# A hybrid layer on one core: the mask inside the scan, w_out prepared in another phase, ten working tiles

## The chip, the cores and the metric

One Trainium2 chip, one of its cores. The program is launched once and runs the whole layer. The metric is the device time of one execution in microseconds, as the median of several runs. TensorE (PE) multiplies and transposes into PSUM, VectorE (DVE) and ScalarE (ACT) work on SBUF and PSUM, GpSimd (POOL) works on SBUF and starts stores, SyncE (SP) starts loads. Each of these engines takes its instructions in the order in which they stand in its own queue.

## The reference

One layer on 2048 positions of width 1024, all float32. A modulated copy of the input, `h = x * (1 + scale) + shift`, goes through one projection into seven groups of 512 columns. Three feed a gated MLP (`u`, `v`, `z_a`), four feed an attention of 8 heads of width 64 (`q`, `k`, `v_b`, `z_b`).

```python
mod = c @ w_ada + b_ada                        # shift, scale, gate
h = x * (1 + scale) + shift
u_a, v_a, z_a, q_b, k_b, v_b, z_b = split(h @ w_in, 7)
out_a = gelu(u_a) * (w_spatial_masked @ layer_norm(gelu(v_a)) + b_s) * silu(z_a)

z = q @ k.T / 8                                # per head, blocks of 128 queries
valid = s_pos < t_pos                          # strictly causal
log_keep = where(valid, -softplus(z), 0)
after = reverse_cumsum(log_keep) - log_keep
w = where(valid, exp(log_sigmoid(z) + after), 0)
out_b = (w @ v_b) * silu(z_b)

y = concat(out_a, out_b) @ w_out
out = layer_norm(2**0.25 * x + (1 + gate) * y, ln_g, ln_b)
```

The attention has no softmax: each key takes a share `sigmoid(z)` of what the keys behind it have left over. In product form `keep = sigmoid(-z)` is what a key leaves, and the running product of `keep` from the newest key to the oldest is what remains.

## The kernel before

**Arithmetic.** Every product of two matrices is made of three matmuls of a high and a low part (`split`, L62: a CAST makes the high part, mostly on ACT, L65, and a subtraction on DVE makes the low part, L68). A step of a projection is three matmuls of 512 columns into one PSUM tile.

**Phases of projection work.** The 2048 positions are four chunks of 512. First `k` and `v_b` of all chunks are made, then `q` and `z_b` of chunk 0 (`qz_chunk`, L226). From there on PE's queue is written as two interleaved streams: the attention, as units, and the rest of the projections, as `pieces` (L899): `q`/`z_b` of chunks 1 to 3 (phases q1, q2, q3), then `v_a` and the spatial mixing (va), then `u` and `z_a` (uz, `gmlp_uz`, L603), then the output projection and the norm (out). The PSUM tiles of these are named `pqz`, `pva`, `puz` and `po` in the rows below.

**An attention unit** (`Unit`, L775) is one head, 256 queries and one chunk of 512 keys. It makes `z` on PE (L805, L806), `kp = sigmoid(-z)` on ACT (L809), for the diagonal chunk a mask on POOL (L812, it writes 1 where the key is not before the query), the running product by a scan on DVE (L820), a transposition on PE into `tr` (L835), the split of that into `wth` and `wtl` (L65, L68), and the product with the values into `pv` (L852, L854), which DVE adds into `ot` (L868). Units are a few steps apart in PE's queue: while one is at its scores, the one before is at its scan and the one before that at its transposition.

**What sets the order.** For PE the order is written out by hand (L944 to L968): a table `rate` (L925) says how many nanoseconds of projection work go beside an attention unit of a given size in each phase. For `k`, `v_b` and the first `q`/`z_b` chunk the orders of SP, DVE and ACT are the written ones too. Elsewhere a scheduler orders the other engines' queues. A tile of a pool takes over the buffer of an earlier one when that one's last reader is done.

**The preparation of w_out** (`prep_out`, L202) is a generator: it loads a block of 128 rows of `w_out` into a `raw` tile by SP (L206), multiplies it by the gate (L213), splits each half into `woh` and `wol`, and stores both parts by POOL into the scratch tensor `wo_d` (L218, L219). There are 8 blocks. `qz_chunk` of chunks 0 and 1 drives it, at the steps listed in L239. The output phase reads `wo_d` back.

**Shared buffers.** `r2` (L103) is a pool of 8 tiles of 128x512: the `sz`, `eh_q`, `el_q` of the q phases, `woh` and `wol`, gelu's two tiles (`gv`, `gt`, `gu`, `gtu`), the mixing result (`mx`, `mxl`), silu's `sga` and the split output `oh`, `ol`. `raw4` (L97) is a pool of 3 tiles of 128x1024, for weights before their split and for rows of `x` later. The gate stays in one of them from the end of the k/v phase to the end of `prep_out`.

**gelu** (L183) copies its PSUM input to SBUF on ACT, squares the PSUM input on ACT (L185), goes on with DVE (L186), a sigmoid on ACT (L187) and DVE (L188).

Of the kernel before, what the change touches and what calls it, by code (L numbers as in the profile page):

```python
# [9 lines left out]
F32 = mybir.dt.float32  # L10
# [25 lines left out]
def layer_kernel(ctx: ExitStack, tc: tile.TileContext, x, c, w_ada, b_ada, w_in, ln_v_g, ln_v_b,  # L36
# [20 lines left out]
    mb_d = [dram.tile([P, 2, 4, CH], F32, name=f"mb_d{i}") for i in range(NC)]  # L57
    wo_d = dram.tile([2, 4, P, 2, 2, 512], F32, name="wo_d")

    store = nc.gpsimd  # L60
# [20 lines left out]
    zero = const.tile([P, 1], F32, name="zero")  # L81
    nc.vector.memset(zero, 0.0)
    cb = const.tile([3 * NB, P], F32, name="cb")
    nc.scalar.dma_start(cb[0:NB], c.rearrange("(b p) -> b p", p=P))
# [18 lines left out]
    def r2(nm, dt=F32, shape=(P, 512)):  # L103
        return right.tile(list(shape), dt, tag="t2", bufs=8, name=nm)

# [77 lines left out]
    def gelu(t, dst, src):  # L183
        nc.scalar.copy(dst, src)
        nc.scalar.activation(t, src, AF.Square)  # L185
        nc.vector.scalar_tensor_tensor(t, t, GC2, dst, op0=ALU.add, op1=ALU.mult)  # L186
        nc.scalar.activation(t, t, AF.Sigmoid, scale=GSC)  # L187
        nc.vector.tensor_tensor(dst, dst, t, op=ALU.mult)  # L188
# [13 lines left out]
    def prep_out():  # L202

        def load(b):
            raw = raw4(f"woraw_{b}", (P, D))
            nc.sync.dma_start(raw, w_out[b * P:(b + 1) * P, :])  # L206
            return raw

        raws = [load(0), load(1)]
        yield 0  # L210
        for b in range(NB):
            raw = raws[b]
            nc.vector.tensor_tensor(raw, raw, gates[0], op=ALU.mult)  # L213
            for i in range(2):
                cs = slice(i * 512, (i + 1) * 512)
                hi, lo = r2(f"woh_{b}_{i}", F32R), r2(f"wol_{b}_{i}", F32R)
                split(hi, lo, raw[:, cs], "act")
                store.dma_start(wo_d[i, b // 2][:, b % 2, 0, :], hi.bitcast(F32))  # L218
                store.dma_start(wo_d[i, b // 2][:, b % 2, 1, :], lo.bitcast(F32))  # L219
            if b + 2 < NB:  # L220
                raws.append(load(b + 2))
            yield 0

    gates, prep, kept = [], [], [None]

    def qz_chunk(ci, hts, w_q, w_z):  # L226
# [9 lines left out]
        tiles += [(w_z, m, True, lambda acc, m=m: put_z(m, acc)) for m in range(4)]  # L236
        for i, ns in enumerate(project(hts, tiles, f"pqz_{ci}", ci > 0, 0 < ci < NC - 1)):
            yield ns
            if ci < 2 and i in ((26, 36, 44, 52, 60), (7, 23, 39, 55))[ci]:  # L239
                yield next(prep[0], 0)  # L240


    with ExitStack() as sa:
# [80 lines left out]
        def make_gate():  # L324
# [16 lines left out]
            gate = raw4("gate", (P, D))  # L341
            gates.append(gate)
            bg = raw4("bgate", (P, D))
            nc.sync.dma_start(bg, b_ada[2 * D:3 * D].unsqueeze(0).broadcast_to([P, D]))
            yield 0
            for i in range(2):
                cs = slice(i * 512, (i + 1) * 512)
                gp = pj(f"gp_{i}")
                nc.tensor.matmul(gp, ones, gacc[:, cs], start=True, stop=True)
                nc.vector.scalar_tensor_tensor(gate[:, cs], gp, 1.0, bg[:, cs], op0=ALU.add, op1=ALU.add)  # L350
                yield 0

        def put_k(ci, m, acc):
# [122 lines left out]
        with tc.manual_schedule(engines={ET.PE, ET.SP, ET.DVE, ET.Activation}):  # L476
# [38 lines left out]
            w_steps = split_steps(w_z, G_ZB, "z", 2)  # L515
            prep.append(prep_out())
            for i, _ in enumerate(qz_chunk(0, hts, w_q, w_z)):
# [85 lines left out]
    def gmlp_uz():  # L603
        w_u = []
        u_steps = split_steps(w_u, G_U, "u")
        for ci in range(NC):
# [38 lines left out]
            for i, ns in enumerate(project(hts, tiles, f"puz_{ci}", ci > 0, ci < NC - 1)):  # L645
                yield ns
                if ci == 0 and i in (6, 8, 18, 25, 28):
                    next(u_steps)

    def turn_a(ci, t, mx):  # L650
# [124 lines left out]
    class Unit:  # L775
# [23 lines left out]
        def scores(self):  # L799
# [8 lines left out]
            for js, w_ in self.rng:  # L808
                nc.scalar.activation(self.kp[:, js, 0:w_], z[:, js, 0:w_], AF.Sigmoid, scale=-ZSC)  # L809
            for j in range(2) if self.diag else ():  # L810
                own = self.kp[:, j, self.wid[j] - P:self.wid[j]]
                nc.gpsimd.affine_select(own, own, pattern=[[-1, P]], compare_op=ALU.is_gt, fill=1.0, base=0,  # L812
                                        channel_multiplier=1)

        def remains(self):

            kp = self.kp
            for j in range(2):
                w_ = self.wid[j]
                nc.vector.tensor_tensor_scan(kp[:, j, 0:w_][:, ::-1], kp[:, j, 0:w_][:, ::-1],  # L820
                                             zero.broadcast_to([P, w_]),
                                             1.0 if self.diag else self.prev.kp[:, j, 0:1],
                                             op0=ALU.mult, op1=ALU.add)

# [74 lines left out]
    def pieces():  # L899
        for ci in range(1, NC):  # L900
# [3 lines left out]
            done.add(ci)  # L904
        yield from prep.pop()
        phase[0] = "va"
# [17 lines left out]
    left = dict(q1=64 * 648, q2=64 * 648, q3=64 * 648, va=128 * 648 + 1800 + 16 * 660, uz=256 * 648 + 32 * 224, out=210 * 648)  # L924
    rate = dict(q1=4.1, q2=3.3, q3=3.3, va=9.0, uz=3.9, out=4.8)  # L925
    stream = with_waiting(pieces())
# [69 lines left out]
```

## Time and profile before

| | |
|---|---|
| median of three runs | 1312.83 us (1311.06 to 1313.43) |
| the profiled execution | 1313.83 us, its span 1312.1 us |
| mean granted TensorE clock | 0.986 of full speed |
| busy share of the span | PE 95%, DVE 72%, ACT 43%, POOL 24% |
| bytes moved | 269.23 MB, 205 GB/s on average |

PE is busy almost everywhere, so a time saved elsewhere counts only where PE waits for it. Matmuls are pipelined: a busy PE may still run at half clock, which the granted clock of a stretch tells. The span has three parts in which PE has real gaps: the start (until about 60 us), the q phases (about 250 to 390 us) and some places between 580 and 775 us; at the end the last norm and store follow the last matmul.

### The profile page before, as it was taken

The page shows a single profiled execution, that of the slowest core. Times are in us where ns is not written, and L with a number is a line of the kernel's source. Part 1 is how long each engine was busy: PE and PEld are TensorE (multiplying, and loading weights), DVE is VectorE, ACT ScalarE, POOL GpSimd, SP SyncE. Part 2 cuts the span into 40 slices and gives each one's busy share as a digit, 9 for nine tenths or more (in the row PEclk, how much of TensorE's full clock was granted, in tenths as well). Part 3 has the DMA queues.
Part 4 walks back from the last instruction along what each step waited for, and adds up shares of the span by engine and source line. Part 5 has one row for each costly group of instructions (what it writes and reads, how often), then busy time and mean ns, then how long its engine had stood idle before and what let it go on. Part 6 is the DMA issues. An engine that isn't in the chain of part 4 may idle for free.

```text
span 1312.1 us, 18828 instructions
## 1 busy us (share of the span) xinstructions
PE 1245.6 (95%) x6678; PEld 1054.7 (80%) x6678; DVE 949.2 (72%) x1362; ACT 561.8 (43%) x1079; POOL 310.6 (24%) x540
## 2 busy tenths in 40 slices
PE   4999999888899999999989989999999999999997
PEld 4788877677678888888868868888888887888885
DVE  6633453446677787878798878888788778878874
ACT  3333222223344454455565545555454433444330
POOL 1344333243222211345431111111001112111111
PEclk9999999999899999999999989999999999999999
DMA  9699876899975764654455653753775976565331
GB/s 318 220 372 320 283 265 203 313 334 306 306 217 167 235 185 134 212 193 153 129 169 177 198 165 102 218 138 110 214 235 137 309 206 185 163 176 168 105 121 49
DMA packets 174623, 269.23 MB, mean 205 GB/s; under 512 B 15008, under 2 KB 107200, under 8 KB 174528
## 3 DMA queue, kind: packets, MB, share of 16 engines
q1 hardware_dynamic: 147216, 178.30, 45.8%
q0 software_dynamic: 27264, 89.70, 19.6%
q8 instruction: 53, 0.87, 0.3%
q14 instruction: 42, 0.34, 0.1%
q10 hardware_dynamic: 48, 0.01, 0.0%
HBM read 180.37 MB, written 83.36 MB: 201 GB/s over the span
## 4 chain that ended last, share of the span: by engine, by line
PE 68%; DVE 10%; issue 9%; DMA 5%; POOL 4%; ACT 2%; SPq 1%; POOLq 0%; DVEq 0%; ACTq 0%
PE puz_False L160 12%; PE pkv L160 11%; PE po L694 10%; PE pqz_True L160 7%; PE tr L835 7%; PE pv L854 4%; PE pv L852 4%; PE z L806 4%; PE z L805 4%; DVE kp L820 2%; PE pva_False L160 2%; DMA woraw<-in_w_out_dram 1%; DMA ht_qz<-ht_d 1%; DVE macc L306 1%; PE pk L160 1%
## 5 line engine op out<-in xcount | busy, mean ns | idle before, releaser
L65 ACT CAST wth<-tr 128x512 fp32r<-128x512 f32 (+2 forms) x352 | 170.8, 486 | 258.1 <-PE tr L835 167.5
L820 DVE TENSOR_TENSOR_SCAN kp<-kp,kp,zero 128x512 f32<-128x512 f32 x192 | 240.0, 1277 | 53.2 <-ACT kp L809 52.9
L68 DVE TENSOR_TENSOR wtl<-tr,wth 128x512 fp32r<-128x512 f32 (+2 forms) x352 | 194.2, 561 | 33.0 <-ACT wth L65 30.2
L694 PE MATMUL po<-wo,mt 128*128 128x512 f32 x744 | 197.5, 402 | 0.7 <-DVE xr L704 0.6
L809 ACT ACTIVATE kp<-z 128x128 f32<-128x128 f32 (+3 forms) x224 | 148.0, 691 | 106.0 <-PE z L806 105.6
L835 PE MATMUL tr<-ident,kp 128*128 128x128 f32 x1088 | 170.7, 277 | 9.1 <-DVE kp L820 8.0
L694 PEld LDWEIGHTS po<-wo,mt 128*128 128x128 f32 x744 | 133.7, 189 | 26.2 <-DVE xr L704 1.6
L835 PEld LDWEIGHTS tr<-ident,kp 128*128 128x128 f32 x1088 | 129.2, 141 | 28.6 <-DVE kp L820 9.5
L852 PE MATMUL pv<-wth,vs 128*128 128x256 f32 x576 | 142.3, 279 | 2.6 <-DVE ot L868 2.6
L854 PE MATMUL pv<-wtl,vs 128*128 128x256 f32 x576 | 141.6, 284 | 0.6 <-DVE wtl L68 0.6
L820 DVE TENSOR_TENSOR_SCAN kp<-kp,zero 128x128 f32<-128x128 f32 (+3 forms) x128 | 103.6, 836 | 34.1 <-POOL kp L812 32.3
L852 PEld LDWEIGHTS pv<-wth,vs 128*128 128x128 f32 x576 | 110.4, 192 | 10.5 <-DVE ot L868 3.9
L805 PE MATMUL z<-ks,qt 128*128 128x512 f32 (+2 forms) x320 | 115.7, 367 | 1.6 <-issue 1.2
L806 PE MATMUL z<-ks,qt 128*128 128x512 f32 (+2 forms) x320 | 117.0, 365 | 0.0
L854 PEld LDWEIGHTS pv<-wtl,vs 128*128 128x128 f32 x576 | 110.5, 192 | 7.2 <-DVE wtl L68 0.8
L812 POOL TENSOR_SCALAR_AFFINE_SELECT kp<-kp 128x128 f32<-128x128 f32 x128 | 49.7, 402 | 214.1 <-ACT kp L809 212.5
L160 PE MATMUL puz_False<-wh_u,ht_uz 128*128 128x512 f32 x192 | 77.1, 422 | 1.8 <-ACT gtu L185 1.8
L160 PE MATMUL pqz_True<-ht_qz,wh_q 128*128 128x512 f32 x192 | 72.0, 413 | 6.9 <-DVE sz L181 3.2
L160 PE MATMUL pqz_True<-ht_qz,wh_z 128*128 128x512 f32 x192 | 74.7, 416 | 3.2 <-DVE el_q L68 3.2
L160 PE MATMUL pkv<-wh_v,hta 128*128 128x512 f32 x224 | 75.8, 402 | 0.5 <-DVE el_k L68 0.5
L160 PE MATMUL puz_False<-wh_za,ht_uz 128*128 128x512 f32 x192 | 75.0, 413 | 0.0
L805 PEld LDWEIGHTS z<-ks,qt 128*128 128x128 f32 x320 | 60.5, 189 | 13.0 <-issue 2.4
(203 smaller groups left out, 2338.9 us busy)
## 6 DMA issues: line engine op xcount, KB each, us to landing
ks<-k_d SPq DMA_DIRECT2D x160, 128.0 KB, 4.1
vs<-v_d SPq DMA_DIRECT2D x80, 256.0 KB, 3.9
qt<-q_d SPq DMA_DIRECT2D x64, 256.0 KB, 4.6
ht_d<-hta POOLq DMA_DIRECT2D x24, 512.0 KB, 5.5
ht_qz<-ht_d SPq DMA_DIRECT2D x24, 512.0 KB, 11.6
ht_va<-ht_d SPq DMA_DIRECT2D x24, 512.0 KB, 4.9
ht_uz<-ht_d SPq DMA_DIRECT2D x24, 512.0 KB, 6.0
wada<-in_w_ada_dram SPq DMA_DIRECT2D x32, 256.0 KB, 6.6
```

The costliest lines, as they stand in the source:

```text
L65: nc.scalar.copy(hi, src)
L68: (sub or nc.vector).tensor_tensor(lo, src, hi.bitcast(F32), op=ALU.subtract)
L160: nc.tensor.matmul(acc, l_, r_, start=(b == 0 and i == 0), stop=(b == NB - 1 and i == 2))
L694: nc.tensor.matmul(acc, ms[l_], w[:, r_, :], start=(b == 0 and i == 0), stop=(b == NB - 1 and i == 2))
L805: nc.tensor.matmul(z[:, j, 0:w_], hd.q[:, 0, qs], hd.k[self.s][:, 0:w_], start=True, stop=False)
L806: nc.tensor.matmul(z[:, j, 0:w_], hd.q[:, 1, qs], hd.k[self.s][:, 0:w_], start=False, stop=True)
L809: nc.scalar.activation(self.kp[:, js, 0:w_], z[:, js, 0:w_], AF.Sigmoid, scale=-ZSC)
L812: nc.gpsimd.affine_select(own, own, pattern=[[-1, P]], compare_op=ALU.is_gt, fill=1.0, base=0, channel_multiplier=1)
L820: nc.vector.tensor_tensor_scan(kp[:, j, 0:w_][:, ::-1], kp[:, j, 0:w_][:, ::-1], zero.broadcast_to([P, w_]), 1.0 if self.diag else self.pr ...
L835: nc.tensor.transpose(tp[:, e, j * P:(j + 1) * P], self.kp[:, j, kb * P:(kb + 1) * P], ident)
L852: nc.tensor.matmul(self.pv[:, cs], hd.v[self.s][:, kb, :], self.wt[0][:, kb, cs], start=self.diag and kb == 0, stop=False)
L854: nc.tensor.matmul(self.pv[:, cs], hd.v[self.s][:, kb, :], self.wt[1][:, kb, cs], start=False, stop=self.s == 0 and kb == self.nkb - 1)
```

## The change

It has five parts.

1. The mask on POOL (L812) goes. A constant tile `least` is 0 where the key is before the query and 1 where not; the diagonal scan's second operation is now a maximum with `least` in place of an addition of zero. As no `keep` exceeds 1, the running product stays at 1 through the masked keys and then goes on as before.
2. `prep_out` is driven from `gmlp_uz` and no longer from `qz_chunk`: its first loads at step 36 of chunk 0, then one call at every 16th step of chunks 1 to 3, which makes the 8 blocks in chunks 1 and 2. The gate waits in a scratch tensor `gate_d` and is loaded into a `raw` tile when it is needed.
3. `r2` has 10 buffers in place of 8.
4. gelu's square reads the copy in SBUF in place of the PSUM tile.
5. In `rate`, q2 and q3 go from 3.3 to 3.2, uz from 3.9 to 4.2 and out from 4.8 to 4.6.

```diff
+    gate_d = dram.tile([1, D], F32, name="gate_d")
...
+    least = const.tile([P, CH], F32, name="least")
+    nc.gpsimd.memset(least, 0.0)
+    nc.gpsimd.affine_select(least[:, CH - P:CH], least[:, CH - P:CH], pattern=[[-1, P]], compare_op=ALU.is_gt, fill=1.0,
+                            base=0, channel_multiplier=1)
...
-        return right.tile(list(shape), dt, tag="t2", bufs=8, name=nm)
+        return right.tile(list(shape), dt, tag="t2", bufs=10, name=nm)
...
-        nc.scalar.activation(t, src, AF.Square)
+        nc.scalar.activation(t, dst, AF.Square)
...
+        gate = raw4("gate_all", (P, D))
+        nc.sync.dma_start(gate, gate_d.broadcast_to([P, D]))
         raws = [load(0), load(1)]
-        yield 0
+        yield
         for b in range(NB):
             raw = raws[b]
-            nc.vector.tensor_tensor(raw, raw, gates[0], op=ALU.mult)
+            nc.vector.tensor_tensor(raw, raw, gate, op=ALU.mult)
...
-            if ci < 2 and i in ((26, 36, 44, 52, 60), (7, 23, 39, 55))[ci]:
-                yield next(prep[0], 0)
+        yield from project(hts, tiles, f"pqz_{ci}", ci > 0, 0 < ci < NC - 1)
...
+            nc.gpsimd.dma_start(gate_d, gate[0:1, :])
...
-        u_steps = split_steps(w_u, G_U, "u")
+        u_steps, wo_steps = split_steps(w_u, G_U, "u"), prep_out()
...
+                if ci == 0 and i == 36 or ci and i % 16 == 9:
+                    next(wo_steps, None)
...
-            for j in range(2) if self.diag else ():
-                own = self.kp[:, j, self.wid[j] - P:self.wid[j]]
-                nc.gpsimd.affine_select(own, own, pattern=[[-1, P]], compare_op=ALU.is_gt, fill=1.0, base=0,
-                                        channel_multiplier=1)
...
-                nc.vector.tensor_tensor_scan(kp[:, j, 0:w_][:, ::-1], kp[:, j, 0:w_][:, ::-1],
-                                             zero.broadcast_to([P, w_]),
-                                             1.0 if self.diag else self.prev.kp[:, j, 0:1],
-                                             op0=ALU.mult, op1=ALU.add)
+                keep = kp[:, j, 0:w_][:, ::-1]
+                if self.diag:
+                    nc.vector.tensor_tensor_scan(keep, keep, least[:, CH - w_:CH][:, ::-1], 1.0, op0=ALU.mult, op1=ALU.max)
+                else:
+                    nc.vector.tensor_tensor_scan(keep, keep, zero.broadcast_to([P, w_]), self.prev.kp[:, j, 0:1],
+                                                 op0=ALU.mult, op1=ALU.add)
...
-        yield from prep.pop()
...
-    rate = dict(q1=4.1, q2=3.3, q3=3.3, va=9.0, uz=3.9, out=4.8)
+    rate = dict(q1=4.1, q2=3.2, q3=3.2, va=9.0, uz=4.2, out=4.6)
```

What this moves in the queues is shown at two places. The first is VectorE's queue where `q` and `z_b` of chunk 0 end. `pqz` is the PSUM tile of a projection, `el_q` and `sz` are what DVE makes of it, `woraw` and `wol` belong to w_out. Before:

```order
L68 TENSOR_TENSOR el_q_3_1989<-pqz_3_True_1945,eh_q_3_1988 128x512
L213 TENSOR_TENSOR woraw_1969<-woraw_1969,gate 128x1024
L68 TENSOR_TENSOR wol_0_2012<-woraw_1969,woh_0_2011 128x512
L68 TENSOR_TENSOR wol_1_2018<-woraw_1969,woh_1_2017 128x512
L181 TENSOR_TENSOR sz_0_2034<-pqz_0_True_1994,sz_0_2034 128x512
L213 TENSOR_TENSOR woraw_1971<-woraw_1971,gate 128x1024
L68 TENSOR_TENSOR wol_0_2056<-woraw_1971,woh_0_2055 128x512
L68 TENSOR_TENSOR wol_1_2062<-woraw_1971,woh_1_2061 128x512
L181 TENSOR_TENSOR sz_1_2078<-pqz_1_True_2038,sz_1_2078 128x512
```

The same place in the changed kernel:

```order
L69 TENSOR_TENSOR el_q_3_1992<-pqz_3_True_1952,eh_q_3_1991 128x512
L186 TENSOR_TENSOR sz_0_2022<-pqz_0_True_1997,sz_0_2022 128x512
L186 TENSOR_TENSOR sz_1_2051<-pqz_1_True_2026,sz_1_2051 128x512
L186 TENSOR_TENSOR sz_2_2080<-pqz_2_True_2055,sz_2_2080 128x512
L186 TENSOR_TENSOR sz_3_2109<-pqz_3_True_2084,sz_3_2109 128x512
L69 TENSOR_TENSOR el_q_0_2170<-pqz_0_True_2128,eh_q_0_2169 128x512
```

Each `sz` stood behind the multiplication of a block of w_out, and now the reads of PSUM stand one behind the other.

The second place is ScalarE's queue where chunk 2 of the uz phase begins. `puz` is the PSUM tile of `u` or `z_a`, `gu` and `gtu` are gelu's tiles, `oh` is the split output of chunk 1, `kp`, `wth` and `hv` belong to attention units. Before:

```order
L65 CAST wth_7_0_1_8472<-tr_7_0_1_1_8494 128x512
L809 ACTIVATE kp_7_1_2_8512<-z_7_1_2_8507 128x384
L809 ACTIVATE kp_7_1_2_8512<-z_7_1_2_8507 128x512
L65 CAST wth_7_0_0_8529<-tr_7_0_0_0_8531 128x512
L65 CAST oh_3_8543<-oT_3_8538 128x512
L184 COPY gu_0_8551<-puz_0_False_8351 128x512
L185 ACTIVATE gtu_0_8552<-puz_0_False_8351 128x512
```

The same place in the changed kernel:

```order
L66 CAST oh_2_8100<-oT_2_8095 128x512
L66 CAST woh_0_8114<-woraw_7641 128x512
L814 ACTIVATE kp_7_0_1_8111<-z_7_0_1_8106 128x1024
L66 CAST woh_1_8120<-woraw_7641 128x512
L66 CAST wth_7_0_2_8141<-tr_7_0_2_0_8143 128x256
L66 CAST wth_7_0_2_8141<-tr_7_0_2_0_8143 128x128
L66 CAST oh_3_8164<-oT_3_8159 128x512
L189 COPY gu_0_8172<-puz_0_False_7980 128x512
L190 ACTIVATE gtu_0_8173<-gu_0_8172 128x512
```

Two casts of w_out have moved in ahead of the copy that frees `puz`, and the square behind that copy reads `gu` and not `puz`. In the built program `gu_0_8172` takes over the buffer of `woh_0_8114`.

## Rows read from the trace of the kernel before

**Rows 1.** Windows, q phases: length, busy of PE, PEld, DVE, ACT, POOL, PEclk, DMA, GB/s

```profile
250.00:390.00 140.00, 119.10 (x591) 98.05 (x590) 82.89 (x137) 51.37 (x136) 44.78 (x94) 0.94 0.96 298
263.05:266.45 3.40, 3.40 (x8) 2.70 (x9) 2.37 (x3) 1.14 (x2) 2.37 (x6) 0.53 0.88 217
307.20:310.20 3.00, 3.00 (x8) 2.43 (x9) 1.88 (x2) 0.00 (x0) 1.58 (x4) 0.51 1.14 262
353.03:358.40 5.37, 5.37 (x19) 4.69 (x20) 1.64 (x4) 1.20 (x3) 0.00 (x0) 0.50 1.04 346
```

**Rows 2.** Waits of PE from 240 to 390: us in total, times, longest

```profile
PE pqz_True L160 <- DVE sz L181: 9.8, 2, 6.6
PE pqz_True L160 <- DVE el_q L68: 4.0, 2, 3.2
PE pqz_True L160 <- DMA ht_qz<-ht_d: 2.9, 2, 1.5
PE pv L852 <- DVE ot L868: 2.6, 3, 1.3
```

**Rows 3.** Waits of DVE in the same stretch

```profile
DVE woraw L213 <- DMA woraw<-in_w_out_dram: 26.8, 5, 12.5
DVE kp L820 <- POOL kp L812: 14.6, 17, 3.4
```

**Rows 4.** DMA from 240 to 370: count, KB each, median us to landing

```profile
DMA packets 19432, 41.06 MB, mean 316 GB/s; under 512 B 2220, under 2 KB 7646, under 8 KB 19423
...
ht_qz<-ht_d SPq DMA_DIRECT2D x13, 512.0 KB, 13.2
...
woraw<-in_w_out_dram SPq DMA_DIRECT2D x8, 512.0 KB, 7.2
wo_d<-woh POOLq DMA_DIRECT2D x16, 256.0 KB, 7.3
```

**Rows 5.** Chain that ended last, 225 to 400: start, length, what

```profile
337.03 15.95 DMA ht_qz<-ht_d
```

**Rows 6.** Groups by line, whole span: busy, mean ns, idle before, releaser

```profile
L820 DVE TENSOR_TENSOR_SCAN kp<-kp,zero 128x128 f32<-128x128 f32 (+3 forms) x128 | 103.6, 836 | 34.1 <-POOL kp L812 32.3
L213 DVE TENSOR_TENSOR woraw<-woraw,gate 128x1024 f32<-128x1024 f32 x8 | 9.8, 1221 | 26.8 <-DMA woraw<-in_w_out_dram 26.8
L68 DVE TENSOR_TENSOR wol<-woraw,woh 128x512 fp32r<-128x512 f32 x16 | 10.4, 688 | 4.7 <-ACT woh L65 3.0 <-DMA wo_d<-woh 1.4
L65 ACT CAST woh<-woraw 128x512 fp32r<-128x512 f32 x16 | 9.3, 619 | 26.1 <-DVE woraw L213 21.3 <-DMA wo_d<-woh 4.1 <-DMA zb_d<-sz 0.7
L187 ACT ACTIVATE gtu<-gtu 128x512 f32<-128x512 f32 x16 | 10.1, 633 | 8.9 <-DVE gtu L186 8.9
L185 ACT ACTIVATE gtu<-puz_False 128x512 f32<-128x512 f32 x16 | 9.8, 611 | 2.0 <-DMA ma_d<-oh 2.0
```

**Rows 7.** Windows of the uz phase

```profile
662.00:690.00 28.00, 23.43 (x134) 19.25 (x134) 25.63 (x36) 18.07 (x36) 10.71 (x12) 1.00 0.53 156
753.00:775.00 22.00, 15.62 (x79) 13.04 (x78) 14.85 (x22) 8.36 (x16) 2.03 (x4) 0.84 0.47 153
767.12:771.10 3.98, 3.98 (x14) 3.30 (x14) 3.09 (x4) 0.58 (x1) 0.00 (x0) 0.50 0.17 66
780.00:940.00 160.00, 160.00 (x939) 139.13 (x938) 136.72 (x187) 84.61 (x162) 20.75 (x36) 1.00 0.57 166
```

**Rows 8.** Waits from 740 to 775

```profile
PE tr L835 <- DVE kp L820: 4.6, 1, 4.6
...
ACT gu L184 <- DMA ma_d<-oh: 3.1, 1, 3.1
```

**Rows 9.** DMA from 690 to 1020, stores of the split output

```profile
ma_d<-oh POOLq DMA_DIRECT2D x14, 256.0 KB, 3.7
```

**Rows 10.** Groups of DVE by line, 780 to 940

```profile
L820 DVE TENSOR_TENSOR_SCAN kp<-kp,kp,zero 128x512 f32<-128x512 f32 x42 | 52.1, 1272 | 12.1 <-ACT kp L809 12.0
L68 DVE TENSOR_TENSOR wtl<-tr,wth 128x512 fp32r<-128x512 f32 (+2 forms) x64 | 36.8, 588 | 5.6 <-ACT wth L65 5.1
```

More of the change, by code (lines that the diff above doesn't have):

```diff
@@ L221, in prep_out @@
                 raws.append(load(b + 2))
-            yield 0
-    gates, prep, kept = [], [], [None]
+            yield
+    kept = [None]
     def qz_chunk(ci, hts, w_q, w_z):
@@ L236, in qz_chunk @@
         tiles += [(w_z, m, True, lambda acc, m=m: put_z(m, acc)) for m in range(4)]
-        for i, ns in enumerate(project(hts, tiles, f"pqz_{ci}", ci > 0, 0 < ci < NC - 1)):
-            yield ns
-            if ci < 2 and i in ((26, 36, 44, 52, 60), (7, 23, 39, 55))[ci]:
-                yield next(prep[0], 0)
+        yield from project(hts, tiles, f"pqz_{ci}", ci > 0, 0 < ci < NC - 1)
     with ExitStack() as sa:
@@ L341, in make_gate @@
             gate = raw4("gate", (P, D))
-            gates.append(gate)
             bg = raw4("bgate", (P, D))
@@ L515, in layer_kernel @@
             w_steps = split_steps(w_z, G_ZB, "z", 2)
-            prep.append(prep_out())
             for i, _ in enumerate(qz_chunk(0, hts, w_q, w_z)):
```

## The prediction

> **What bounds the kernel now.** I read the windows first, then PE's waits, then the groups by line. In the windows the reader is to compare PE's busy time with the length. In the long stretch of the uz phase PE is busy for all of its 160.00 us at the full clock [rows 7]: there the kernel is bound by PE, and a saved microsecond on another engine is worth nothing. From 250 to 390 us PE is busy for 119.10 of 140.00 us, so 20.9 us are idle [rows 1]. The waits of the same stretch name them: 9.8 us for `sz` and 4.0 us for `el_q`, both DVE's reads of PSUM, 2.9 us for the hidden states `ht_qz`, 2.6 us for `ot` [rows 2], and 1.6 us that is left for small ones. [...] PE's queue keeps its work and nearly its order, and PE is the bound on both sides of the stretch, so I count what goes here one to one.
>
> Why DVE was late: its queue stands still for 26.8 us for blocks of `w_out`, once for 12.5 us [rows 3], with `sz` and `el_q` behind the waiting multiplication, and PE behind these, as PSUM has two tiles for projections. DMA is full there (0.96 busy [rows 1]); the 8 loads and 32 stores of w_out are 8 x 0.5 + 32 x 0.25 = 12 of the 41.06 MB moved from 240 to 370 us [rows 4].
>
> **w_out out of the q phases.** The waits for `sz` and `el_q` go with their cause: 13.8 us, and the first two slow stretches behind them, (3.40 + 3.00) / 2 = 3.2 us. That is 17.0 us, and I count all of it. What is late next is a transfer: one `ht_qz` took 15.95 us from issue [rows 5], against a median of 13.2 [rows 4], and PE needs these tiles some 11 to 13 us after they are issued (it waited 1.5 us at the longest). Without the 12 MB the queue ahead of it is shorter by three tenths, which brings 15.95 to about 11. So of the 2.9 us, the 1.6 us and the third slow stretch (2.7 us), 7.2 us in all, I count 6. Bounds: 0 and 7.2.
>
> **The mask.** 128 POOL instructions go. DVE waited 14.6 us for them in this stretch [rows 3], mostly where it was idle anyway; what PE saw of it is within the 2.6 us for `ot`. I count 1 us, between 0 and 2.6. The diagonal scan now takes a maximum with a tile, which no row shows. Its own group has 836 ns for 320 elements on average [rows 6]. At best it stays (nothing gets shorter, the elements are as many). At worst the second tile costs what a plain pass over two inputs costs, 688 ns x 320/512 = 430 ns [rows 6], and 128 of them add 55 us to DVE, of which only what falls in a full DVE would count. I take 0, as the addition already is a second operation of this row.
>
> [...]
>
> The tile `least` costs POOL two instructions at the start, where PE waits for the first loads. `gate_d` costs one small store and one load of 0.5 MB, in a phase with DMA to spare (0.57 [rows 7]).
>
> **w_out into the uz phase.** Each of 8 blocks costs DVE 1.22 us for the product and 2 x 0.688 us, ACT 2 x 0.619 us [rows 6], and four stores by POOL: 20.8 us of DVE and 9.9 us of ACT in all, over chunks 1 and 2, some 165 us. ACT has 84.61 of 160.00 us busy and takes it. DVE has 136.72 [rows 7]. By the table `rate`, attention leaves this phase: PE's queue has 226 transposes of 128 columns in chunks 1 and 2 before and 214 now, 5% fewer, which takes 5% of the scans and splits, (52.1 + 36.8) x 0.053 = 4.7 us [rows 10]. DVE then stands at 136.7 + 20.8 - 4.7 = 152.8 of 160 us, 95%. The cover is thin. Lower bound 0: at 85% PE did not wait at all. Upper bounds: if no idle time of DVE can be used, 20.8 us. If PE loses the share that it lost from 662 to 690 us, where DVE was busy for 25.63 of 28.00 us and PE for 23.43 [rows 7], 16% of 160 us is 26. That row had weights to split just ahead of their use, which here nobody waits for until the out phase, so I stay nearer to the 160 us row and take 5 us.
>
> What queues behind a waiting instruction: SP's load of block b + 2 waits for block b's buffer, with keys and values behind it, but these are issued a unit ahead. In SP's queue of the q phase, six of these loads stood ahead of the first keys and now three loads of `v_a`'s weights do.
>
> **Two more tiles, and the square.** From 753 to 775 us PE is idle for 22.00 - 15.62 = 6.4 us and at half speed for another 3.98 [rows 7], so 8.4 us are lost. It begins with ACT, which waits 3.1 us to copy a PSUM tile, as its target still holds a split output on its way to memory; PE then waits 4.6 us for the scan behind that [rows 8]. With 10 buffers such a reuse comes later, and the square no longer needs the PSUM tile (0.5 us earlier free). But 32 tiles of w_out join the pool. I count 5 us, between 0 and 8.4. The square costs ACT 633 in place of 611 ns [rows 6], 32 times, 0.7 us under cover.
>
> The out phase takes some of the attention that left: DVE rises there, PE has the same work in sum. I put 1 us against it, between 0 and 3.
>
> **Sum.** Gains 17.0 + 6 + 1 + 5 = 29, costs 5 + 1 = 6: 23 us. The profiled execution took 1313.8 us with a span of 1312.1; 1313.8 - 23 = 1290.8. The profiled one stands 1.0 us above the median shown, so the median should be about 1290.
>
> **Rivals.** [...]
>
> (b) DVE becomes the bound in chunks 1 and 2. With 12 us lost there in place of 5, and 3 of the 6 us of the transfer gained, it is 23 - 7 - 3 = 13, or 1300; with all 20.8 us lost and nothing gained from the transfer, 23 - 15.8 - 6 = 1, which is no change. For it: the row from 662 to 690 us.
>
> (c) Slower: the stall of 753 us at every block. If ACT has to wait for a w_out store before it can copy a PSUM tile, each such place costs 8.4 us [rows 7, 8]; 23 / 8.4 = 2.7, so from three of them on the gain is gone, and with four it is 1290 + 4 x 8.4 = 1324. For it: in ACT's queue a copy of `gu` stands five instructions behind the `woh` whose buffer it takes. Against it: it is the only reuse of that closeness that I found among the stored tiles, and stores in this phase land in 3.7 us where w_out's took 7.3 [rows 4, 9].
>
> [...]
>
> (d) The change does not do what it says: PE in the q phases meets another wait of the same size, the loads of keys and hidden states above all, as DMA stays full. Then 1312. Against it: the waits that go have their cause in w_out by name.
>
> **Chances.** The forecast with its near range, 1282 to 1296: 0.58. (a) 0.13. (b) 0.16. (c) 0.07. (d) 0.06. A difference under 0.2%, 2.6 us, is about what a measurement of this kernel cannot tell from none. Faster is forecast, (a) and (b), 0.87; within 0.2% most of (d), 0.05; slower (c) and a rest, 0.08. The range of 8 in 10 leaves out (c), (d) and the ends of (a) and (b): 1276 to 1305.
>
> **What would show it.** Right: PE idle from 245 to 365 us in the new profile at 5 us or less, the clock at 1.00 there, no wait of `pqz` for `sz`; DVE at 93 to 97% in chunks 1 and 2 of the uz phase, PE idle there under 6 us; mean diagonal scan within 3% of 836 ns. Wrong: PE waits for `ht_qz` over 4 us (then the transfer term fails); ACT waits for `wo_d` stores ahead of `gu` or `sga` (then (c)); PE waits for `tr` or `pv` from DVE all through chunks 1 and 2 (then (b)).

## The result and the profile after

The changed kernel takes 1289.7 us in the median of four runs (1289.29 to 1292.41), the one before 1311.9 (1309.23 to 1313.43) beside it: a ratio of 0.9843, 95% interval 0.9822 to 0.9864. The forecast was 1290 with 1276 to 1305. The profiled execution has a span of 1288.1 us, 24.0 less than before.

The windows below cut both spans at the same four pieces of work: the q phases (with the first `q`/`z_b` chunk), va, uz, out. First the kernel before, as length, then busy time of PE, PEld, DVE, ACT and POOL, granted clock, DMA share, GB/s:

```profile
221.90:517.80 295.90, 275.00 (x1454) 231.36 (x1452) 196.28 (x296) 125.14 (x285) 78.27 (x159) 0.97 0.77 242
517.80:656.80 139.00, 135.76 (x727) 115.50 (x726) 111.53 (x167) 73.38 (x166) 60.59 (x85) 0.99 0.58 177
656.80:1019.30 362.50, 351.54 (x2045) 303.89 (x2045) 303.69 (x414) 193.75 (x363) 56.21 (x93) 0.99 0.57 171
1019.30:1312.10 292.80, 280.62 (x1526) 238.48 (x1524) 228.34 (x320) 102.04 (x170) 40.89 (x83) 0.99 0.54 163
```

The same four of the changed kernel, and behind them the stretch of [rows 1] and chunks 1 and 2 of the uz phase:

```profile
222.80:493.60 270.80, 268.86 (x1469) 228.87 (x1467) 178.22 (x279) 120.30 (x276) 39.00 (x69) 1.00 0.69 218
493.60:632.30 138.70, 136.11 (x738) 115.78 (x738) 112.92 (x169) 77.94 (x167) 59.49 (x72) 1.00 0.57 181
632.30:982.00 349.70, 339.57 (x1960) 292.72 (x1959) 301.74 (x416) 190.63 (x360) 57.83 (x85) 1.00 0.69 207
982.00:1288.10 306.10, 289.16 (x1585) 245.26 (x1583) 238.29 (x333) 108.17 (x182) 35.13 (x65) 0.99 0.52 160
...
250.00:390.00 140.00, 138.90 (x751) 118.19 (x750) 84.13 (x145) 56.76 (x150) 17.85 (x33) 1.00 0.75 232
...
721.50:893.00 171.50, 165.56 (x951) 142.68 (x950) 152.58 (x214) 93.91 (x180) 34.34 (x57) 0.99 0.72 224
```

The q phases are 25.1 us shorter: 19.0 us less idle time of PE (20.9 to 1.9), and the mean granted clock is 1.00 in place of 0.97. The uz phase is 12.8 us shorter and the out phase 13.3 longer, which is mostly attention moved by the table: uz idles 10.1 us (11.0 before), out 16.9 (12.2). Here a phase's length misleads when work has moved; its idle time and its clock don't.

What answers to [rows 2] and [rows 4]: waits of PE from 240 to 390 (us in total, times, longest), then DMA from 240 to 370 (count, KB each, median us to landing), changed kernel:

```profile
PE z L810 <- DMA qt<-q_d: 0.9, 1, 0.9
PE pv L855 <- DVE ot L871: 0.2, 1, 0.2
```

```profile
DMA packets 19212, 33.30 MB, mean 256 GB/s; under 512 B 1952, under 2 KB 9120, under 8 KB 19203
...
ht_qz<-ht_d SPq DMA_DIRECT2D x8, 512.0 KB, 6.7
```

The waits for `sz`, `el_q` and `ht_qz` are gone, and hidden states land in 6.7 us in place of 13.2. Of the groups by line of the changed kernel, those that answer to [rows 6] (busy, mean ns, idle before and its releasers):

```profile
L823 DVE TENSOR_TENSOR_SCAN kp<-kp,least 128x128 f32<-128x128 f32 (+3 forms) x128 | 100.4, 820 | 15.2 <-ACT kp L814 14.5
L190 ACT ACTIVATE gtu<-gu 128x512 f32<-128x512 f32 x16 | 10.1, 634 | 2.2 <-DMA wo_d<-woh 1.0 <-DMA ma_d<-ol 0.9
L220 DVE TENSOR_TENSOR woraw<-woraw,gate_all 128x1024 f32<-128x1024 f32 x8 | 9.8, 1220 | 9.4 <-DMA woraw<-in_w_out_dram 7.5 <-issue 1.9
```

The scan with a maximum takes what the scan with an addition took, 820 ns against 836 [rows 6]. The product by the gate still waits for its load, 7.5 us in sum. That wait reaches PE. Waits of PE for DVE in the uz phase of the changed kernel, nearly all of its 10.1 us there:

```profile
PE pv L855 <- DVE ot L871: 5.3, 4, 2.1
PE tr L838 <- DVE kp L825: 3.9, 3, 2.4
```

DVE's and then PE's queue of the changed kernel around the longest one (start, duration, line, operation, in brackets the idle time before and its end):

```profile
832.42 1.22 DVE L220 TENSOR_TENSOR woraw<-woraw,gate_all 128x1024 f32<-128x1024 f32 x1 [4.13 <-DMA woraw<-in_w_out_dram]
...
836.54 2.45 DVE L825 TENSOR_TENSOR_SCAN kp<-kp,kp,zero 128x512 f32<-128x512 f32 x2
```

```profile
837.88 0.33 PE L838 MATMUL tr<-ident,kp 128*128 128x128 f32 x1 [2.44 <-DVE kp L825]
839.05 0.55 PE L838 MATMUL tr<-ident,kp 128*128 128x128 f32 x3 [0.85 <-DVE kp L825]
```

SP issued this load at 825.08, and the product stood at the head of DVE's queue from 828.3. The scan that PE needed stood six instructions behind it, and DVE had no gap between the two. With 0.57 us for `ot` at 834.76, which stood behind the product too, PE loses 3.9 us at this place, and in the 7 us from 836 on the granted clock is 0.76 on average.

### The profile page after: what moved, and what is told of

It reads as the page before. It is cut to its first block, busy times and chain, and to the rows that moved or that the text cites. A ratio compares the mean times of both kernels' runs of the same rounds, so it can differ in the third digit from the quotient of the medians.

```text
span 1288.1 us, 18465 instructions
## 1 busy us (share of the span) xinstructions
PE 1236.7 (96%) x6678; PEld 1048.2 (81%) x6678; DVE 940.6 (73%) x1362; ACT 564.5 (44%) x1079; POOL 267.6 (21%) x415
## 4 chain that ended last, share of the span: by engine, by line
PE 69%; DVE 13%; issue 9%; POOL 3%; DMA 3%; ACT 3%; SPq 0%; POOLq 0%; DVEq 0%; ACTq 0%
PE pqz_True L165 13%; PE pkv L165 11%; PE po L699 9%; PE puz_False L165 9%; PE tr L838 6%; PE pv L857 4%; PE pva_False L165 4%; PE z L810 3%; PE pv L855 3%; PE z L811 3%; DVE kp L825 3%; DVE wtl L69 2%; DVE macc L310 1%; PE pk L165 1%; PE xT L274 1%
## 5 line engine op out<-in xcount | busy, mean ns | idle before, releaser
L855 PEld LDWEIGHTS pv<-wth,vs 128*128 128x128 f32 x576 | 109.4, 190 | 13.8 <-DVE ot L871 7.7
L823 DVE TENSOR_TENSOR_SCAN kp<-kp,least 128x128 f32<-128x128 f32 (+3 forms) x128 | 100.4, 820 | 15.2 <-ACT kp L814 14.5
L165 PE MATMUL puz_False<-wh_u,ht_uz 128*128 128x512 f32 x192 | 74.5, 413 | 0.0
L810 PEld LDWEIGHTS z<-ks,qt 128*128 128x128 f32 x320 | 60.2, 188 | 14.8 <-ACT kp L814 3.0
L811 PEld LDWEIGHTS z<-ks,qt 128*128 128x128 f32 x320 | 60.3, 188 | 10.8
```

Of the source, the lines that this page charges most:

```text
L165: nc.tensor.matmul(acc, l_, r_, start=(b == 0 and i == 0), stop=(b == NB - 1 and i == 2))
L810: nc.tensor.matmul(z[:, j, 0:w_], hd.q[:, 0, qs], hd.k[self.s][:, 0:w_], start=True, stop=False)
L811: nc.tensor.matmul(z[:, j, 0:w_], hd.q[:, 1, qs], hd.k[self.s][:, 0:w_], start=False, stop=True)
L823: nc.vector.tensor_tensor_scan(keep, keep, least[:, CH - w_:CH][:, ::-1], 1.0, op0=ALU.mult, op1=ALU.max)
L855: nc.tensor.matmul(self.pv[:, cs], hd.v[self.s][:, kb, :], self.wt[0][:, kb, cs], start=self.diag and kb == 0, stop=False)
```

## The experiments

Twelve kernels, each timed beside the kernel before; a ratio is to the runs of that kernel in the same session, whose median was 1309.4 to 1311.9 us, so ratios compare better than medians. Lengths of the phases, and in brackets PE's idle time in them, are from one profiled execution of each; the cuts are those of the windows above. A few us in one phase of one execution say little: e6, for which no difference to the changed kernel is measured, has a uz phase 3.0 us longer.

| kernel | median us | ratio to before, 95% | span | q phases | uz | out |
|---|---|---|---|---|---|---|
| before | 1311.9 | | 1312.1 | 295.9 (20.9) | 362.5 (11.0) | 292.8 (12.2) |
| changed | 1289.7 | 0.9843 (0.9822 to 0.9864) | 1288.1 | 270.8 (1.9) | 349.7 (10.1) | 306.1 (16.9) |
| e1 move only | 1308.7 | 0.9989 (0.9974 to 1.0004) | 1307.1 | 273.3 (4.4) | 379.6 (20.7) | 292.6 (12.0) |
| e2 all but the move | 1302.4 | 0.9942 (0.9922 to 0.9962) | 1299.0 | 292.2 (16.4) | 340.9 (2.8) | 305.3 (16.2) |
| e3 8 buffers | 1297.0 | 0.9904 (0.9884 to 0.9925) | 1296.6 | 269.6 (1.1) | 358.2 (14.3) | 306.4 (17.4) |
| e4 mask on POOL | 1298.3 | 0.9919 (0.9898 to 0.9939) | 1295.0 | 273.5 (4.0) | 352.7 (11.1) | 306.9 (16.7) |
| e5 old rates | 1290.3 | 0.9851 (0.9821 to 0.9881) | 1289.6 | 267.4 (0.9) | 369.6 (15.0) | 292.8 (12.1) |
| e6 square from PSUM | 1290.9 | 0.9860 (0.9833 to 0.9888) | 1290.0 | 269.6 (1.1) | 352.7 (10.7) | 306.1 (17.1) |
| e7 product on POOL | 1284.1 | 0.9812 (0.9786 to 0.9838) | 1285.2 | 270.0 (1.1) | 346.7 (6.4) | 306.6 (16.4) |
| e8 slow in q | 1293.8 | 0.9884 (0.9856 to 0.9911) | 1294.8 | 286.0 (9.9) | 340.9 (2.8) | 306.5 (16.3) |
| e9 slow in q, POOL | 1289.2 | 0.9849 (0.9823 to 0.9875) | 1286.6 | 278.8 (6.7) | 339.2 (2.8) | 306.1 (17.0) |
| e10 two loads (six blocks left out) | 1282.9 | 0.9800 (0.9775 to 0.9825) | 1281.1 | 270.3 (1.5) | 343.0 (5.8) | 306.3 (17.2) |
| e11 late product | 1288.5 | 0.9832 (0.9810 to 0.9854) | 1287.4 | 270.8 (1.9) | 347.7 (8.3) | 306.4 (17.3) |
| e12 late, slow in q | 1286.9 | 0.9825 (0.9805 to 0.9845) | 1282.7 | 276.5 (5.8) | 339.2 (2.8) | 306.2 (17.0) |

**e1: the move alone.** The four other parts undone; what is left is:

```diff
-            if ci < 2 and i in ((26, 36, 44, 52, 60), (7, 23, 39, 55))[ci]:
-                yield next(prep[0], 0)
...
+                if ci == 0 and i == 36 or ci and i % 16 == 9:
+                    next(wo_steps, None)
```

> The kernel before with one part alone: the preparation of w_out moved to the u/z phase (gate_d included); mask on POOL, 8 buffers, square from PSUM and the old rates stay. Theory (the q phases gain because w_out leaves them, and nothing else is needed for it): PE idle in the q phases falls from 20.9 us to 4 or less at a clock of 1.00, and the time is 1290 to 1299, since the stall at 753 us (8.4 us with its slow stretch) may stay and w_out adds reuses to 8 buffers. Rival (the freed POOL and the new rates carry a good part of the q phases): PE idle there stays at 8 us or more, the time at 1302 or above.

The q phases did nearly what the theory said: 22.6 us shorter, idle 4.4 where it had 4 or less. But the uz phase is 17.1 us longer, and no difference to before is measured; the time lies in the rival's range, though not for the rival's reason. The theory had the place of the gain right and missed its price. Waits of PE and of ACT in e1's uz phase:

```profile
PE puz_False L161 <- ACT gtu L186: 5.8, 2, 3.8
PE tr L838 <- DVE kp L825: 5.6, 6, 2.0
PE pv L855 <- DVE ot L871: 4.9, 4, 2.0
```

```profile
ACT gu L185 <- DMA ma_d<-oh: 5.1, 1, 5.1
...
ACT gu L185 <- DMA wo_d<-wol: 2.9, 2, 1.7
ACT gu L185 <- DMA wo_d<-woh: 2.6, 1, 2.6
```

With 8 buffers ACT stands behind stores of w_out and of the split output, and PE behind ACT (5.8 us). PE's waits for DVE's scans and `ot` are larger still, 10.5 us.

**e2: the other four without the move.** The lines of e1 the other way round.

> The changed kernel with w_out's preparation put back into the q phases; the four other parts stay. Theory: PE idle in the q phases is again 17 to 22 us, waits for sz and el_q above 9 us; the stall at 753 us is gone, so the time is 1303 to 1309. Rival (mask, buffers and rates repair the q phases too): PE idle there under 12 us, the time under 1300.

The time is just below the theory's range and above the rival's. In the q phases PE idles 16.4 us, just under the theory's 17, and the waits of DVE and PE there are those that it named:

```profile
DVE woraw L217 <- DMA woraw<-in_w_out_dram: 26.9, 7, 12.3
```

```profile
PE pqz_True L164 <- DVE sz L185: 7.1, 2, 6.4
PE pqz_True L164 <- DVE el_q L68: 2.4, 1, 2.4
```

The 26.8 us of [rows 3] are back, though spread a little less badly for PE (waits for `sz` and `el_q` 9.5 in place of 13.8). What the theory had not seen is the uz phase: without w_out the other parts leave it 2.8 us idle in place of 11.0. Beside the changed kernel, e2 gives the two prices of the move: 292.2 - 270.8 = 21.4 us gained in q, 349.7 - 340.9 = 8.8 us paid in uz.

**e3: 8 buffers.** One number in the changed kernel:

```diff
-        return right.tile(list(shape), dt, tag="t2", bufs=10, name=nm)
+        return right.tile(list(shape), dt, tag="t2", bufs=8, name=nm)
```

> The changed kernel with 8 r2 buffers in place of 10. Theory: with w_out's 32 tiles in the pool, 8 buffers bring ACT's waits for stores back (3 us or more in sum in the u/z phase, against 2.5 with 10) and the time is 1294 to 1300. Rival (the buffers do nothing, the stall of before was one unlucky reuse): 1288 to 1292.

As the theory said. The two longest of ACT's waits for stores in its uz phase:

```profile
ACT gu L189 <- DMA ma_d<-oh: 4.7, 1, 4.7
ACT gu L189 <- DMA wo_d<-woh: 3.8, 1, 3.8
```

In the changed kernel all such waits for `ma_d` and `wo_d` come to 2.8 us. The two buffers are worth 8.5 us of span, all of it in the uz phase (358.2 against 349.7), and the intervals of the two ratios do not meet.

**e4: the mask on POOL.**

```diff
+            for j in range(2) if self.diag else ():
+                own = self.kp[:, j, self.wid[j] - P:self.wid[j]]
+                nc.gpsimd.affine_select(own, own, pattern=[[-1, P]], compare_op=ALU.is_gt, fill=1.0, base=0,
+                                        channel_multiplier=1)
...
-nc.vector.tensor_tensor_scan(keep, keep, least[:, CH - w_:CH][:, ::-1], 1.0, op0=ALU.mult, op1=ALU.max)
+nc.vector.tensor_tensor_scan(keep, keep, zero.broadcast_to([P, w_]), 1.0, op0=ALU.mult, op1=ALU.add)
```

> The changed kernel with the mask as 128 POOL instructions again and the addition of zero in the diagonal scan. Theory (DVE waits for the mask mostly where it is idle anyway): 1289 to 1293, DVE's wait for the mask 20 to 35 us in sum with no more than 2 us of it seen by PE. Rival (the mask sits in the chain from z to the transposition, and ahead of POOL's stores): 1294 to 1300. Diagonal scan 836 ns, the changed kernel's 820 ns: equal within 3%.

The rival is right, by the time and by DVE's wait, which is over the theory's 35 us. DVE's wait for the mask, whole span:

```profile
DVE kp L823 <- POOL kp L813: 36.1, 45, 4.5
```

The span is 6.9 us longer (8.6 by the medians), 2.7 in q, 3.0 in uz and the rest in small pieces; the intervals of the two ratios do not meet, but how the loss divides among the phases is not sure. PE waits in q for `ot` (2.2 us in place of 0.2). The longest of these waits, in DVE's queue and then in PE's:

```profile
339.72 1.23 DVE L823 TENSOR_TENSOR_SCAN kp<-kp,zero 128x512 f32<-128x512 f32 x1 [1.44 <-POOL kp L813]
340.98 0.43 DVE L871 TENSOR_TENSOR ot<-pv,hv 64x256 f32<-64x256 f32 x1
```

```profile
341.46 0.39 PE L855 MATMUL pv<-wth,vs 128*128 128x256 f32 x1 [1.62 <-DVE ot L871]
```

`ot` stands behind a scan that waits for the mask. That is how such a wait is missed: PE's row names the instruction it needed, not the one that instruction stood behind. The scan takes 834 ns with the addition, 820 with the maximum.

**e5: the old rates, and e6: the square from PSUM.**

```diff
-    rate = dict(q1=4.1, q2=3.2, q3=3.2, va=9.0, uz=4.2, out=4.6)
+    rate = dict(q1=4.1, q2=3.3, q3=3.3, va=9.0, uz=3.9, out=4.8)
```

> The changed kernel with the old table (q2 and q3 3.3, uz 3.9, out 4.8). Theory A (the new rates take attention, and so DVE work, out of the u/z phase, which w_out's work has filled): with the old ones that phase idles 14 us or more in place of 10.1, the out phase 12 in place of 16.9, and the time is 1289 to 1293. Theory B (the rates only move work; the out phase's 4.7 us of new idle time is their whole effect): the u/z phase keeps 10 us of idle time, the out phase falls to 12, and the time is 1284 to 1287.

```diff
-        nc.scalar.activation(t, dst, AF.Square)
+        nc.scalar.activation(t, src, AF.Square)
```

> The changed kernel with gelu's square reading PSUM again. Theory (the PSUM tile is freed after the copy anyway, the square stands right behind it): 1288 to 1292, the u/z phase idle 9 to 11 us. Rival (a PSUM tile that waits for two reads holds PE where ACT stands behind a store, as in the 1.8 us wait for gtu of the kernel before): 1293 to 1297 with PE waiting for gtu 2 us or more.

Theory A of e5 and the theory of e6 hold. The rates take 4.9 us of idle time out of uz and put 4.8 into out: no difference is measured. Nor is one for the square.

**e7: the product on POOL, and e10: two loads.** Two ways to take the wait for the load out of DVE's queue. The second leaves all of DVE's work in, but six blocks of w_out out, so it is a probe and no version of the kernel:

```diff
-            nc.vector.tensor_tensor(raw, raw, gate, op=ALU.mult)
+            nc.gpsimd.tensor_tensor(raw, raw, gate, op=ALU.mult)
```

> The changed kernel with w_out's product by the gate on POOL in place of DVE. Takes 9.8 us of product and 7.5 us of waiting for the loads from DVE's queue. Theory A (DVE's queue behind the waiting product is what costs the u/z phase its 8.8 us): idle there falls from 10.1 to 6 or less and the time to 1283 to 1287. Theory B (the cost is the pool of tiles and the stores; POOL's queue now holds stores behind a waiting product): idle 10 or more, 1289 to 1300.

```diff
-                raws.append(load(b + 2))
+                raws.append(raw)
```

> The changed kernel with two blocks of w_out loaded in place of eight: each product takes a tile that has long been in SBUF (the later six blocks are the first two multiplied again, so six blocks of w_out and what the output phase makes of them are left out). DVE's work is the same, its wait for the loads (7.5 us) goes. Theory A (the wait is what costs the u/z phase): idle there 6 us or less as with the product on POOL, time 1282 to 1286. Theory B (DVE's work of 20.8 us is what costs): idle 9 to 11 us, time 1288 to 1291.

Theory A in both, by the time; e7 idles 6.4 us, a little over its bound. The uz phases of e7 and then of e10:

```profile
631.90:978.60 346.70, 340.28 (x1960) 294.21 (x1958) 304.51 (x408) 190.93 (x360) 77.92 (x93) 0.99 0.70 209
```

```profile
631.80:974.80 343.00, 337.20 (x1961) 291.68 (x1959) 301.81 (x416) 190.54 (x360) 57.80 (x85) 1.00 0.68 202
```

DVE is as busy in e10 as in the changed kernel (301.81 and 301.74 us), yet PE idles 5.8 us in place of 10.1 and the phase is 6.7 us shorter. So of the 8.8 us that the move costs there, some three quarters go with the loads and not with DVE's work. The trace says where: the 3.9 us around 837 us are gone in e10, and the two shorter places, near 684 and 752 us, stay (1.1 and 1.9 us). In e7 DVE is even busier (304.51 us), and PE waits 5.3 us for DVE's scans and `ot` in place of 9.2. e10 also moves 3 MB less; e11 was to tell that apart.

**e8, e9: in the q phases, but slowly.** e8 drives the changed kernel's `prep_out` from `qz_chunk`, and e9 adds the edit of e7:

```diff
+            if ci and i % 16 == 8:
+                next(prep[0], None)
...
-                if ci == 0 and i == 36 or ci and i % 16 == 9:
-                    next(wo_steps, None)
```

> The changed kernel with w_out's preparation in the q phases again, but slowly: one block at every 16th step of chunks 1 to 3, in place of five calls late in chunk 0 and four in chunk 1. Theory (the q phases lost 20 us because the 12 MB came within 100 us of full DMA; DVE has room there): the q phases idle 6 us or less, the u/z phase 3 to 4 us as with the preparation back in q, and the time is 1278 to 1284, better than both kernels. Rival (any w_out block in the q phases makes the multiplication wait for its load and PE behind it): q idle 10 us or more, the time 1288 or above.

> The slow preparation in the q phases (one block at every 16th step of chunks 1 to 3) with the product by the gate on POOL. Theory (what costs the q phases is DVE's queue standing behind a product that waits for its load, 22.6 us with the product on DVE; DMA at 0.80 is not the cause): the q phases idle 3 us or less in 273 us, the u/z phase 3 us as before, the time 1276 to 1282. Rival (the 12 MB themselves delay keys, hidden states or POOL's stores of q and z_b): the q phases idle 6 us or more, with PE waiting for a DMA or for el_q and sz, the time 1284 or above.

e8 is nearer to its rival (idle 9.9 us, time 1293.8), and e9's rival holds. In e8's q phases a wait of DVE and what PE waits for, then in e9's a wait of POOL:

```profile
DVE woraw L220 <- DMA woraw<-in_w_out_dram: 22.6, 7, 6.5
```

```profile
PE pv L856 <- DVE ot L872: 9.1, 4, 4.3
```

```profile
POOL woraw L220 <- DMA woraw<-in_w_out_dram: 35.8, 7, 7.2
```

A slower pace does not help a product that is queued right behind its own load: 22.6 us of waiting for 8 blocks in place of 26.9. On POOL the wait stands ahead of the stores instead, and PE once waits 3.8 us for a `qt` that is read back from such a store's target. That POOL's queue is the cause of this is not shown: e12, whose POOL has no product, has the same wait (4.3 us).

**e11, e12: the product behind the buffer.** The product is written into the tile of the low part, which comes free late, so that the scheduler can't put it right behind the load; e12 does this with the pace of e8.

```diff
-            nc.vector.tensor_tensor(raw, raw, gate, op=ALU.mult)
...
+                prod = lo.bitcast(F32)
+                nc.vector.tensor_tensor(prod, raw[:, cs], gate[:, cs], op=ALU.mult)
+                split(hi, lo, prod, "act")
```

> The changed kernel with the product by the gate in two halves that go into the tile of the low part, so that a product cannot stand in DVE's queue before that tile is free; in that queue it now stands right ahead of its own split and no longer behind its load. All eight blocks are loaded and all work is done (DVE 16 x 0.69 in place of 8 x 1.22 us). Theory (the wait for the load is what costs the u/z phase): DVE's wait for w_out under 1 us, the u/z phase idle 6 us or less, the time 1282 to 1286. Rival (the six loads and their DMA are what the kernel with two loads had gained from): idle 9 us or more, the time 1288 to 1292.

> The same late product with the slow preparation in the q phases (one block at every 16th step of chunks 1 to 3). Theory: with no product that waits for its load, on DVE or on POOL, the q phases idle 3 us or less and the u/z phase 3 us, the time 1277 to 1282, the best of all. Rival (DMA at 0.80 in the q phases makes PE wait for ht_qz or q_d in any case): q idle 5 us or more, the time 1284 to 1290.

In e11 DVE's wait for w_out is gone, but idle time falls only to 8.3 us, between the two expectations, and the time of 1288.5 lies in the rival's range: no gain over the changed kernel is measured. PE's waits for DVE there:

```profile
PE pv L856 <- DVE ot L872: 1.9, 1, 1.9
PE tr L839 <- DVE kp L826: 1.4, 3, 0.7
```

These are 3.3 us in place of 9.2, and none around 837 us, with all eight loads in. What came in their place is another stall. ACT now stands behind stores of w_out again, 9.3 us for two copies of `gu`; here the longer one in its queue, and what PE waited for behind it:

```profile
747.16 0.59 ACT L189 COPY gu<-puz_False 128x512 f32<-128x512 f32 x1 [5.27 <-DMA wo_d<-woh]
...
749.98 1.03 ACT L815 ACTIVATE kp<-z 128x1024 f32<-128x1024 f32 x1
```

```profile
751.05 0.33 PE L811 MATMUL z<-ks,qt 128*128 128x128 f32 x1 [3.85 <-ACT kp L815]
```

Without this one stall of 3.9 us the phase would idle 8.3 - 3.9 = 4.4 us with all eight loads in place. That speaks for the wait and against the 3 MB as e10's gain, but it is a subtraction and no run: the stall covers the place near 752 us at which e10 and e7 idle 1.9 us, so 4.4 may be too little, and the time of e11 doesn't show the gain.

In e12 DVE's wait for the load is gone too. PE's waits in its q phases:

```profile
PE z L812 <- DMA qt<-q_d: 4.3, 1, 4.3
PE pv L857 <- DVE ot L873: 0.7, 2, 0.4
```

The rival of e12 holds: idle 5.8 us, time 1286.9, PE waiting for a DMA. But e12 and e8 differ by the late product alone (in two halves, into another tile), with the same pace, loads and stores, and e12 is faster: PE's wait for `ot` falls from 9.1 to 0.7 us, the q phases are 9.5 us shorter, and the intervals of the two ratios do not meet. This is the clearest test that a product queued right behind its load is what held PE.

No version with all the work done is clear of the changed kernel. e7 is the nearest: 1284.1 (1283.34 to 1287.03) against 1289.7 (1289.29 to 1292.41), but in another session, and the intervals of the ratios still overlap.

## Why the prediction was right, and what in it was not

The time came out within 1 us of the forecast, and the largest term within 2; three smaller ones were off and in part made up for each other, so that the total came so close is partly luck. The prices found by undoing one part at a time (21.4 - 8.8 + 8.5 + 6.9 = 28.0) are 4 us over the 24.0 gained, as the parts depend on each other.

e5 shows the same by phase. With the old table its phases hold the attention of those before, so their lengths can be compared: q is 28.5 us shorter, uz 7.1 longer, out the same. The prediction had the uz phase even (5 gained, 5 lost) and the q phases at 24, the mask included. So 4.5 us more came in q than it counted, and 7.1 us were lost in uz that it had not.

- **w_out out of the q phases, 17 + 6 = 23 us.** Right: 21.4 (e2 beside the changed kernel) and 22.6 (e1 beside before), and the rows named are the ones that went; PE idles 1.1 us from 245 to 365, where 5 or less was to show it. That the queue behind the product is what matters is shown by e2, where the waits are back, and by e8 beside e12, where the late product alone takes them away. The 3.2 us in the 17.0, and the 2.7 us in what was counted as 6, are half of the time of the windows at a granted clock of 0.53, 0.51 and 0.50 [rows 1], an estimate of the author; no run shows these terms by themselves. What the runs show in their place: for 1469 matmuls each, PE is busy for 275.81 us in the q phases of e2, at a mean granted clock of 0.98, and for 268.86 us in those of the changed kernel, at 1.00, so of the 21.4 us 14.5 are idle time and 6.9 are busy time.
- **w_out into uz, 5 us.** Mis-sized, 8.8, and for another reason. The prediction priced a DVE that is 95% full. It is 152.58 / 171.50 = 89% busy in chunks 1 and 2, below the 93% that was to show it right, though PE idles 5.9 us there, just under the 6 named. e10, with the same work of DVE, idles 3.0 us more than e2, which has none of it. Most of the cost is the mechanism that the prediction itself had read in the q phases [rows 3]: the product stands behind its load and DVE's queue behind the product. The rest, some 2 us, stays in e10 and may be DVE's work. The step that failed is "What queues behind a waiting instruction": it followed SP's load and forgot DVE's product, though block b + 2 is loaded only when block b's buffer is free, so the wait moves with the code.
- **Two more tiles, 5 us.** The mechanism was right [rows 8]; the size is 8.5 us (e3), just over the bound of 8.4, as the 32 tiles of w_out would have made new stalls. With 8 buffers the move costs 17.1 us in uz (e1), with 10 it costs 8.8. The two parts can't be added: the move is worth almost nothing alone and about 13 us (1302.4 to 1289.7; 10.9 by the spans) with the others.
- **The mask, 1 us.** Mis-sized, 6.9 us, outside its bounds of 0 to 2.6. These were read in one stretch alone and from PE's rows for `ot`; the mask is in every phase. The scan's price was right at 0: 820 against 836 ns. That it would be, because the addition already is a second operation, was the prediction's reading; these two numbers agree with it, and no other run tests it.
- **The square: nothing** (e6). **The out phase, 1 us against:** its idle time grows by 4.7, and uz has 4.9 less for the same table (e5); the sum of both is nothing.

Of the rivals, (a), a gain above the forecast, is out (uz still idles 10.1 us) and (d) too. (b) had the right victim: PE waits for `kp` and `ot` there, but DVE is not the bound: in e7 it is busier, and PE idles less. (c) is the mechanism of e1, e3 and e11, where ACT does stand behind w_out stores; one such place cost PE 3.9 us of idle time in e11, where the 8.4 held 6.4. In the changed kernel itself ACT's waits for w_out's stores are 1.9 us in sum. With DVE 89% busy in chunks 1 and 2, w_out's stores land in uz in 4.5 and 5.6 us, less than the 7.3 us of [rows 4]:

```profile
wo_d<-woh POOLq DMA_DIRECT2D x16, 256.0 KB, 4.5
wo_d<-wol POOLq DMA_DIRECT2D x16, 256.0 KB, 5.6
```

## What to carry to other kernels

When work is moved to fill a quieter phase, its waits move with it: look where its first instruction that depends on a transfer stands in an in-order queue, and what that queue holds next, before counting busy shares. An engine's row names the instruction it needed; read on in the other engine's queue for what stood ahead of that. Price a pool's size together with the work that will use it, and an edit that is in every phase over the whole span and not in the stretch that drew attention to it. A sum that comes out right shows little about its terms: here undoing one part at a time showed three wrong sizes inside a right total.

## What the runs showed of the hardware that was not expected

In e7 some of DVE's instructions stretch while POOL multiplies. POOL and DVE of e7, two places:

```profile
803.08 2.71 POOL L220 TENSOR_TENSOR woraw<-woraw,gate_all 128x1024 f32<-128x1024 f32 x1 [6.20 <-DMA woraw<-in_w_out_dram]
...
853.11 2.38 POOL L220 TENSOR_TENSOR woraw<-woraw,gate_all 128x1024 f32<-128x1024 f32 x1 [4.19 <-DMA woraw<-in_w_out_dram]
```

```profile
802.65 4.22 DVE L823 TENSOR_TENSOR_SCAN kp<-kp,least 128x384 f32<-128x384 f32 x2
...
853.21 2.56 DVE L823 TENSOR_TENSOR_SCAN kp<-kp,least 128x128 f32<-128x128 f32 x1
```

The same shapes in the changed kernel, the first on average:

```profile
L823 DVE TENSOR_TENSOR_SCAN kp<-kp,least 128x128 f32<-128x128 f32 x32 | 13.4, 417 | 3.6 <-ACT kp L814 3.3
...
840.70 2.06 DVE L823 TENSOR_TENSOR_SCAN kp<-kp,least 128x384 f32<-128x384 f32 x2
```

The 128x128 scan begins 0.10 us behind the product's start and ends 0.28 us behind its end; in the changed kernel this shape takes 417 ns on average. The pair at 802.65, a scan of 384 elements and one of 512, takes 4.22 us where such a pair takes 2.06. These scans read two tiles in SBUF, `kp` and `least`; by what way the product holds them up is not shown. So the product on POOL gave DVE none of its 9.8 us back: in e7's uz phase DVE is busy 304.51 us with eight instructions fewer, in the changed kernel 301.74. Whether the mask's instructions on POOL held DVE up in the same way was not tried; in the kernel before, which has the mask on POOL and adds, the 128x128 scan takes 481 ns on average in place of 417, which may be that.
